# Pairing the stores of a batched matrix product: 6 KB runs by column-tiled products, and x issued two batches ahead

## The chip, the cores and the metric

One core of a Trainium2 chip. The metric is the device time of one execution in microseconds (us). Times are medians; every set of experiments has its own runs of the kernel before on the same chip, since chips and moments differ by about 0.1 us.

## The reference

```python
def setup_inputs():
    batch, dim_i, dim_j, dim_k = 32, 256, 512, 384
    # x: (32, 256, 512) float32,  y: (32, 512, 384) float32
def reference(x, y):
    return np.einsum('bij,bjk->bik', x, y).astype(np.float32)
```

x is 16.8 MB, y 25.2 MB and the result 12.6 MB. All of it has to pass the DMA engines once (the profile before: HBM read 41.94 MB, written 12.58 MB).

## The kernel before

x of four batches is loaded in one DMA (16 KB per partition), y of each batch in one DMA (6 KB per partition). PE, the matrix engine, transposes x; ACT and DVE, the scalar and the vector engine, cast the transposes and y to fp16; PE multiplies; ACT and DVE copy the products out, and the result of each batch leaves in a DMA of its own: 128 partitions, two rows of 1.5 KB each, a run of 3 KB. All DMAs are issued by SP, the sync engine, in program order (`eng` below is SP for every batch). The 16 DMA engines work a DMA off in packets; here each run of contiguous bytes is one packet (32 stores of 128 runs give the 4,096 packets of 3 KB in the trace). Each DMA adds 16 packets of 4 bytes, called completions here (1,152 for the 72 DMAs of the trace, with a median record of 9 ns).

```python
    def load(b):
        if b % Q == 0:                       # Q = 4
            x_of[b // Q] = x_pool.tile([P, R, J], F32, name="x_sb")
            keep(nc.sync.dma_start(out=x_of[b // Q],
                 in_=x[b : b + Q].rearrange("g (p r) j -> (g p) r j", r=R)))
        y_of[b] = y_pool.tile([P, NJ, K], F32, name="y_sb")
        keep(nc.sync.dma_start(out=y_of[b], in_=y[b].rearrange("(q t) k -> q t k", q=P)))
    ...
    def multiply(b):                         # two tiles of 128 rows, four products each
        ...
                keep(nc.tensor.matmul(ps_of[b][e], xt_sb[:, t, e].rearrange("c p h -> c (p h)"),
                                      y_r[:, t], start=(t == 0), stop=(t == NJ - 1)))
    ...
    def store(b):
        keep(eng.dma_start(out=out[b].rearrange("(m e) k -> m e k", m=P), in_=o_of.pop(b)))
    ...
    for s in range(B + 2):                   # one batch a stage
        if s + ahead < B: load(s + ahead)
        if s >= 2:        collect(s - 2)
        if 1 <= s <= B:   multiply(s - 1)
        if s < B and s % Q == 0: transpose(s // Q)
        if s < B:         round_y(s)
        if s >= 2:        store(s - 2)
```

## Time and profile before

| | before |
|---|---|
| time, median (range) | 136.25 us (136.09 to 136.34) |
| span of the profiled run (its device time) | 134.7 us (136.52 us) |
| busy: PE, ACT, DVE | 66%, 59%, 55% |
| DMA queue: packets, share of 16 engines | 10,368, 97.9% |
| mean DMA rate over the span | 405 GB/s |

Two more views of the page are needed later: the groups of instructions (busy us, mean ns of one, idle time before and who ended it) and the DMA issues (count, KB each, median us from issue to landing).

```profile
L94 ACT CAST xt_sb<-t_ps 128x512 f16<-128x512 f32 x32 | 39.8, 1350 | 44.0 <-PE t_ps L84 43.9
L92 DVE CAST xt_sb<-t_ps 128x512 f16<-128x512 f32 x32 | 40.1, 1323 | 40.3 <-PE t_ps L84 40.2
...
L115 PE MATMUL o_ps<-y_r,xt_sb 128*128 128x384 f16 x256 | 46.3, 342 | 14.9 <-ACT y_r L102 14.9
...
y_sb<-in_y_dram SPq DMA_DIRECT2D x32, 768.0 KB, 15.1
x_sb<-in_x_dram SPq DMA_DIRECT2D x8, 2048.0 KB, 14.2
out_dram<-o_sb SPq DMA_DIRECT2D x32, 384.0 KB, 14.1
```

The casts of the transposes take 1.3 us each, the products come in 256 instructions of 128 weight columns, and a DMA lands some 14 to 15 us after its issue, which is a queue that is always full (97.9% of 16 engines' span).

### The profile page before, as it was taken

What the parts mean: (1) busy time and instruction counts of PE and PEld (TensorE: products, weight loads), DVE (VectorE), ACT (ScalarE), POOL (GpSimd) and SP (SyncE); (2) the same over time, 40 slices, a digit from 0 to 9 for tenths busy, and PEclk for the clock granted to TensorE, in tenths of its full rate; (3) what the DMA queues carried; (4) which work ended last, traced back from release to release, by engine and by line L of the source; (5) the groups of instructions that cost most, each with busy time, mean ns of one, the idle gap of its engine ahead of it and who ended that gap; (6) DMA issues with size and microseconds to landing.
All of it is one profiled execution on the core that took longest, in us unless ns stands there. A gap on an engine that the chain in (4) does not pass through costs nothing.

```text
span 134.7 us, 1539 instructions
## 1 busy us (share of the span) xinstructions
PE 89.5 (66%) x512; PEld 66.6 (49%) x512; DVE 73.7 (55%) x128; ACT 80.1 (59%) x129; POOL 0.7 (1%) x6
## 2 busy tenths in 40 slices
PE   0049499769677908949794983949459492794920
PEld 0048368644564408925492543936259360793510
DVE  0008855975397503873489340796228870378720
ACT  3007994996299602795479650699218990179910
POOL 2000000000000000000000000000000000000000
PEclk9999999999999985686999599599995999559995
DMA  5999999999999999999999999999999999999992
GB/s 131 399 413 423 447 412 416 416 434 414 404 422 451 425 399 424 421 435 437 400 416 430 438 425 410 421 418 454 407 409 425 433 440 402 421 421 413 412 410 84
DMA packets 10375, 54.62 MB, mean 405 GB/s; under 512 B 1152, under 2 KB 1152, under 8 KB 9344
## 3 DMA queue, kind: packets, MB, share of 16 engines
q1 hardware_dynamic: 10368, 54.53, 97.9%
q8 instruction: 4, 0.07, 0.2%
q14 instruction: 3, 0.02, 0.0%
HBM read 41.94 MB, written 12.58 MB: 405 GB/s over the span
## 4 chain that ended last, share of the span: by engine, by line
DMA 79%; PE 8%; ACT 5%; DVE 2%; issue 2%; SPq 1%; DVEq 0%
DMA y_sb<-in_y_dram 30%; DMA x_sb<-in_x_dram 27%; DMA out_dram<-o_sb 21%; PE o_ps L115 4%; PE t_ps L84 4%; ACT xt_sb L94 2%; ACT y_r L102 2%; DVE xt_sb L92 1%; DVE y_r L104 1%; DVE o_sb L130 0%; SPq L69 0%; ACT o_sb L128 0%; SPq L63 0%; DVEq L130 0%
## 5 line engine op out<-in xcount | busy, mean ns | idle before, releaser
L94 ACT CAST xt_sb<-t_ps 128x512 f16<-128x512 f32 x32 | 39.8, 1350 | 44.0 <-PE t_ps L84 43.9
L92 DVE CAST xt_sb<-t_ps 128x512 f16<-128x512 f32 x32 | 40.1, 1323 | 40.3 <-PE t_ps L84 40.2
L84 PE MATMUL t_ps<-identity,x_sb 128*128 128x128 f32 x256 | 43.4, 340 | 24.5 <-DMA x_sb<-in_x_dram 24.3
L115 PE MATMUL o_ps<-y_r,xt_sb 128*128 128x384 f16 x256 | 46.3, 342 | 14.9 <-ACT y_r L102 14.9
L84 PEld LDWEIGHTS t_ps<-identity,x_sb 128*128 128x128 f32 x256 | 41.1, 216 | 27.8 <-issue 26.4
L115 PEld LDWEIGHTS <-xt_sb 128*128 128x128 f16 x256 | 26.2, 102 | 34.2 <-issue 19.9
L102 ACT CAST y_r<-y_sb 128x384 f16<-128x384 f32 x64 | 30.2, 527 | 0.6 <-DMA y_sb<-in_y_dram 0.6
L130 DVE COPY o_sb<-o_ps 128x384 f32<-128x384 f32 x32 | 17.8, 556 | 15.1 <-PE o_ps L115 15.1
L104 DVE CAST y_r<-y_sb 128x384 f16<-128x384 f32 x64 | 19.9, 354 | 0.4 <-DMA y_sb<-in_y_dram 0.4
L128 ACT COPY o_sb<-o_ps 128x384 f32<-128x384 f32 x32 | 15.4, 483 | 3.8 <-PE o_ps L115 3.8
L94 ACT ACT_TABLE_LOAD x1 | 1.3, 1283 | 0.7 <-PEq L168 0.7
masks.py:199 POOL TENSOR_SCALAR_AFFINE_SELECT identity<-identity 128x128 f32<-128x128 f32 x1 | 0.3, 294 | 0.1
masks.py:197 POOL MEMSET identity<- 128x128 f32 x1 | 0.2, 205 | 0.3 <-POOLq L168 0.3
L168 POOL MEMSET const-bfloat16-1.0<- 128x1 bf16 x1 | 0.1, 102 | 0.0
L168 POOL MEMSET const-uint8-127<- 128x1 uint8 x1 | 0.1, 102 | 0.0
L168 POOL MEMSET const-float32-0.0<- 128x1 f32 x1 | 0.1, 99 | 0.2 <-issue 0.2
L168 POOL MEMSET const-float32-1.0<- 128x1 f32 x1 | 0.1, 99 | 0.0
## 6 DMA issues: line engine op xcount, KB each, us to landing
y_sb<-in_y_dram SPq DMA_DIRECT2D x32, 768.0 KB, 15.1
x_sb<-in_x_dram SPq DMA_DIRECT2D x8, 2048.0 KB, 14.2
out_dram<-o_sb SPq DMA_DIRECT2D x32, 384.0 KB, 14.1
```

What stands on the lines that cost most here:

```text
L84: nc.tensor.transpose(t_ps[:, h].rearrange("c g p -> c (g p)"), x_sb[:, h * NI + e, t::NJ], identity,)
L92: keep(nc.vector.tensor_copy(dst, t_ps))
L94: keep(nc.scalar.copy(dst, t_ps))
L102: keep(nc.scalar.copy(yr_of[b][:, t], y_sb[:, t]))
L104: keep(nc.vector.tensor_copy(yr_of[b][:, t], y_sb[:, t]))
L115: nc.tensor.matmul(ps_of[b][e], xt_sb[:, t, e].rearrange("c p h -> c (p h)"), y_r[:, t], start=(t == 0), stop=(t == NJ - 1),)
L128: keep(nc.scalar.copy(o_of[b][:, e], ps_of[b][e]))
L130: keep(nc.vector.tensor_copy(o_of[b][:, e], ps_of[b][e]))
L168: nc = _bacc.Bacc("TRN2", target_bir_lowering=False, num_devices=1)
```

## The change

The intent: put the results of two batches side by side in the partitions (64 rows of one batch in partitions 0 to 63, 64 rows of the other in 64 to 127), so that one partition holds four rows of one batch, and a store of two batches has 6 KB runs. For that a product may give only 64 rows, so it is column-tiled: the two batches use the two halves of PE's columns. x is issued two batches ahead of the y that needs it, and transposed in two halves.

```diff
+G = 2
-LAG = 8
+LAG = 4                      # now counts pairs of batches
...
+    M = P // G               # 64 rows of each batch
+    NE = I // M
...
-        for e in range(NI):
-                    nc.tensor.matmul(ps_of[b][e], xt_sb[:, t, e] ..., y_r[:, t], ...)
+        for e in range(NE):
+            o_ps = opsum_pool.tile([P, K], F32, name="o_ps")
+            for t in range(NJ):
+                for g in range(G):
+                    nc.tensor.matmul(o_ps[g * M : (g + 1) * M],
+                        xt_sb[:, t, e, a * PQ : (a + 1) * PQ] ..., y_r[:, g, t], ...)
...
-        keep(eng.dma_start(out=out[b].rearrange("(m e) k -> m e k", m=P), in_=o_of.pop(b)))
+            nc.sync.dma_start(
+                out=out[u * G : (u + 1) * G].rearrange("g (m e) k -> (g m) e k", e=NE),
+                in_=o_of.pop(u))
...
+        if (u + 1) * G % Q == 0 and u + 1 < U:
+            load_x((u + 1) * G // Q)        # two batches ahead of its y
...
-    for s in range(B + 2):
+    for s in range(U + 2):                  # one pair of batches a stage
```

More of the change, by code (lines that the diff above doesn't have):

```diff
@@ L15 @@
 Q = 4
-LAG = 8
-ON_ACT = ()
+G = 2
+LAG = 4
 @with_exitstack
@@ L33 @@
     _, _, K = y.shape
-    NI = I // P
+    M = P // G
+    NE = I // M
     NJ = J // P
-    R = Q * NI
     PQ = P // Q
+    R = I // PQ
+    H = R // NE
+    U = B // G
     const_pool = ctx.enter_context(tc.tile_pool(name="const", bufs=1))
     x_pool = ctx.enter_context(tc.tile_pool(name="x_pool", bufs=3))
-    y_pool = ctx.enter_context(tc.tile_pool(name="y_pool", bufs=10))
-    yr_pool = ctx.enter_context(tc.tile_pool(name="yr_pool", bufs=4))
+    y_pool = ctx.enter_context(tc.tile_pool(name="y_pool", bufs=5))
+    yr_pool = ctx.enter_context(tc.tile_pool(name="yr_pool", bufs=2))
     xt_pool = ctx.enter_context(tc.tile_pool(name="xt_pool", bufs=2))
-    o_pool = ctx.enter_context(tc.tile_pool(name="o_pool", bufs=10))
+    o_pool = ctx.enter_context(tc.tile_pool(name="o_pool", bufs=5))
     tpsum_pool = ctx.enter_context(tc.tile_pool(name="tpsum", bufs=4, space=bass.MemoryType.PSUM))
@@ L57, with load_x, load @@
     x_of, y_of, yr_of, xt_of, ps_of, o_of = {}, {}, {}, {}, {}, {}
-    def load(b):
-        if b % Q == 0:
-            x_of[b // Q] = x_pool.tile([P, R, J], F32, name="x_sb")
+    def load_x(q):
+        x_of[q] = x_pool.tile([P, R, J], F32, name="x_sb")
+        keep(
+            nc.sync.dma_start(
+                out=x_of[q],
+                in_=x[q * Q : (q + 1) * Q].rearrange("g (p r) j -> (g p) r j", r=R),
+            )
+        )
+    def load(u):
+        if u == 0:
+            load_x(0)
+        if (u + 1) * G % Q == 0 and u + 1 < U:
+            load_x((u + 1) * G // Q)
+        y_of[u] = y_pool.tile([P, G, NJ, K], F32, name="y_sb")
+        for g in range(G):
@@ L62, in load @@
             keep(
                 nc.sync.dma_start(
-                    out=x_of[b // Q],
-                    in_=x[b : b + Q].rearrange("g (p r) j -> (g p) r j", r=R),
-                )
-            )
-        y_of[b] = y_pool.tile([P, NJ, K], F32, name="y_sb")
-        keep(nc.sync.dma_start(out=y_of[b], in_=y[b].rearrange("(q t) k -> q t k", q=P)))
-    def transpose(q):
-        x_sb = x_of.pop(q)
-        xt_of[q] = xt_pool.tile([P, Q, NJ, NI, PQ, Q], MM_DT, name="xt_sb")
-        n = 0
-        for t in range(NJ):
-            for e in range(NI):
-                t_ps = tpsum_pool.tile([P, Q, Q, PQ], F32, name="t_ps")
-                for h in range(Q):
-                    keep(
-                        nc.tensor.transpose(
-                            t_ps[:, h].rearrange("c g p -> c (g p)"),
-                            x_sb[:, h * NI + e, t::NJ],
-                            identity,
-                        )
-                    )
-                dst = xt_of[q][:, :, t, e].rearrange("c g p h -> c h g p")
+                    out=y_of[u][:, g],
@@ new lines, in load, with transpose @@
+                    in_=y[u * G + g].rearrange("(q t) k -> q t k", q=P),
+                )
+            )
+    def transpose(q, half):
+        x_sb = x_of[q]
+        if half == 0:
+            xt_of[q] = xt_pool.tile([P, NJ, NE, Q * PQ, H], MM_DT, name="xt_sb")
+        n = 0
+        for t in range(half * NJ // 2, (half + 1) * NJ // 2):
+            for e in range(0, NE, 2):
+                t_ps = tpsum_pool.tile([P, 2, H, Q * PQ], F32, name="t_ps")
+                for f in range(2):
+                    for h in range(H):
+                        keep(
+                            nc.tensor.transpose(
+                                t_ps[:, f, h], x_sb[:, h * NE + e + f, t::NJ], identity
+                            )
+                        )
+                dst = xt_of[q][:, t, e : e + 2].rearrange("c f p h -> c f h p")
@@ L95, in transpose @@
                 n += 1
-    def round_y(b):
-        y_sb = y_of.pop(b)
-        yr_of[b] = yr_pool.tile([P, NJ, K], MM_DT, name="y_r")
-        for t in range(NJ):
-            if t % 2 == 0:
-                keep(nc.scalar.copy(yr_of[b][:, t], y_sb[:, t]))
-            else:
-                keep(nc.vector.tensor_copy(yr_of[b][:, t], y_sb[:, t]))
-    def multiply(b):
-        xt_sb, y_r = xt_of[b // Q][:, b % Q], yr_of.pop(b)
-        ps_of[b] = [
-            opsum_pool.tile([P, K], F32, name=f"o_ps_{e}", tag="o_ps")
-            for e in range(NI)
-        ]
-        for t in range(NJ):
-            for e in range(NI):
-                keep(
-                    nc.tensor.matmul(
-                        ps_of[b][e],
-                        xt_sb[:, t, e].rearrange("c p h -> c (p h)"),
-                        y_r[:, t],
-                        start=(t == 0),
-                        stop=(t == NJ - 1),
-                    )
-                )
@@ L124, in collect, with round_y @@
-    def collect(b):
-        o_of[b] = o_pool.tile([P, NI, K], F32, name="o_sb")
-        for e in range(NI):
-            if e % 2 == 0:
-                keep(nc.scalar.copy(o_of[b][:, e], ps_of[b][e]))
-            else:
-                keep(nc.vector.tensor_copy(o_of[b][:, e], ps_of[b][e]))
-        del ps_of[b]
-    def store(b):
-        eng = nc.scalar if b in ON_ACT else nc.sync
-        keep(eng.dma_start(out=out[b].rearrange("(m e) k -> m e k", m=P), in_=o_of.pop(b)))
+    def round_y(u):
+        y_sb = y_of.pop(u)
+        yr_of[u] = yr_pool.tile([P, G, NJ, K], MM_DT, name="y_r")
+        for g in range(G):
+            for t in range(NJ):
+                if t % 2 == 0:
+                    keep(nc.scalar.copy(yr_of[u][:, g, t], y_sb[:, g, t]))
+                else:
+                    keep(nc.vector.tensor_copy(yr_of[u][:, g, t], y_sb[:, g, t]))
@@ new lines, in multiply @@
+    def multiply(u):
+        xt_sb, y_r = xt_of[u * G // Q], yr_of.pop(u)
+        ps_of[u] = []
+        for e in range(NE):
+            o_ps = opsum_pool.tile([P, K], F32, name="o_ps")
+            ps_of[u].append(o_ps)
+            for t in range(NJ):
+                for g in range(G):
+                    a = (u * G + g) % Q
+                    keep(
+                        nc.tensor.matmul(
+                            o_ps[g * M : (g + 1) * M],
+                            xt_sb[:, t, e, a * PQ : (a + 1) * PQ].rearrange("c p h -> c (p h)"),
+                            y_r[:, g, t],
+                            start=(t == 0),
+                            stop=(t == NJ - 1),
+                        )
+                    )
@@ new lines, in collect, with store @@
+    def collect(u):
+        o_of[u] = o_pool.tile([P, NE, K], F32, name="o_sb")
+        for e in range(NE):
+            if e % 2 == 0:
+                keep(nc.scalar.copy(o_of[u][:, e], ps_of[u][e]))
+            else:
+                keep(nc.vector.tensor_copy(o_of[u][:, e], ps_of[u][e]))
+        del ps_of[u]
+    def store(u):
+        keep(
+            nc.sync.dma_start(
+                out=out[u * G : (u + 1) * G].rearrange("g (m e) k -> (g m) e k", e=NE),
+                in_=o_of.pop(u),
+            )
+        )
@@ L138 @@
     ahead = LAG - 2
-    for b in range(ahead):
-        load(b)
-    for s in range(B + 2):
-        if s + ahead < B:
+    for u in range(ahead):
+        load(u)
+    for s in range(U + 2):
+        if s + ahead < U:
             load(s + ahead)
+        if s == 0:
+            transpose(0, 0)
+            transpose(0, 1)
         if s >= 2:
             collect(s - 2)
-        if 1 <= s <= B:
+        if 1 <= s <= U:
             multiply(s - 1)
-        if s < B and s % Q == 0:
-            transpose(s // Q)
-        if s < B:
+        if s < U:
@@ L151 @@
             round_y(s)
+        for half in range(2):
+            q = (s + 1 - half) * G // Q
+            if (s + 1 - half) * G % Q == 0 and 0 < q < B // Q:
+                transpose(q, half)
         if s >= 2:
```

## The prediction

> **What bounds the kernel now.** I began with the page: the busy shares, the slices and the DMA queue.
>
> ```profile
> PE 89.5 (66%) x512; PEld 66.6 (49%) x512; DVE 73.7 (55%) x128; ACT 80.1 (59%) x129; POOL 0.7 (1%) x6
> ...
> DMA  5999999999999999999999999999999999999992
> GB/s 131 399 413 423 447 412 416 416 434 414 404 422 451 425 399 424 421 435 437 400 416 430 438 425 410 421 418 454 407 409 425 433 440 402 421 421 413 412 410 84
> DMA packets 10375, 54.62 MB, mean 405 GB/s; under 512 B 1152, under 2 KB 1152, under 8 KB 9344
> ...
> q1 hardware_dynamic: 10368, 54.53, 97.9%
> ...
> DMA 79%; PE 8%; ACT 5%; DVE 2%; issue 2%; SPq 1%; DVEq 0%
> ```
>
> No compute engine is busy for more than 66% of the span. The DMA engines show 9 in every slice from the second to the last but one, at 400 to 454 GB/s, and the packets of the one queue take 97.9% of 16 engines' span: 0.979 x 134.7 = 131.9 us of a 134.7 us span. So DMA **throughput** bounds the kernel. The chain of waits agrees (79% DMA). What remains outside is small: the packet records of the trace show the first packet at 1.74 us and the last packet's end at 133.58 us.
>
> Then I asked why the compute waits do not matter. The waits by engine:
>
> ```profile
> ACT xt_sb L94 <- PE t_ps L84: 43.9, 16, 8.7
> DVE xt_sb L92 <- PE t_ps L84: 40.2, 18, 9.8
> ...
> PE t_ps L84 <- DMA x_sb<-in_x_dram: 24.3, 7, 8.7
> ```
>
> PE waits 24.3 us for x, in 7 stretches of up to 8.7 us, and ACT and DVE wait for PE in turn. These waits look large, but while PE is idle the DMA row still shows 9: an idle engine below a saturated queue costs nothing. The table of stretches carries the number that matters here, how fast a queue full of one kind of packet runs:
>
> ```profile
> 9.00:13.00 4.00, 3.81 (x21) 3.62 (x19) 2.77 (x3) 2.02 (x2) 0.00 (x0) 1.00 1.02 427
> 124.00:130.00 6.00, 4.97 (x31) 2.77 (x29) 3.53 (x9) 4.50 (x11) 0.00 (x0) 1.00 1.03 414
> ```
>
> The last two columns are DMA share and GB/s. From 9 to 13 us only y moves, in 6 KB runs: 427 GB/s. From 124 to 130 us almost only stores move, in 3 KB runs: 414 GB/s. Both are full, at 1.02 and 1.03. The 3 KB stores are thus about 3% less efficient per byte, and they are 12.58 of 54.5 MB.
>
> [...] Its packet records give medians of 121 ns for 3,072 B, 234 ns for 6,144 B and 611 ns for 16,384 B. The slope is (611 - 234) / 10,240 = 0.0368 ns per byte, or 27.2 GB/s per engine and 435 for sixteen, and the rest is 234 - 0.0368 x 6,144 = 8 ns per packet. The same two numbers give 113 + 8 = 121 ns for a 3 KB store, so stores and loads obey one law. [...] Its weight loads for the products take 102 ns and lie under the products.
>
> **The change part by part.**
>
> *Stores.* Before: 32 DMAs of 128 runs of 3 KB, 4,096 packets, 4,096 x 121 ns / 16 = 31.0 us of all engines. After: 16 DMAs of 128 runs of 6 KB, 2,048 packets, 2,048 x 234 ns / 16 = 30.0 us. Saved: 1.0 us. The stretches give the same: 12.58 MB / 414 - 12.58 MB / 427 = 30.4 - 29.5 = 0.9 us. Sixteen DMAs fewer also take 16 x 16 = 256 of the 4-byte completion packets away, at 9 ns: 256 x 9 / 16 = 0.14 us. The sum of packet time goes from 131.95 to about 130.9 us. Bytes and load runs (16 KB for x, 6 KB for y) stay. This part lies wholly on the path, because the path is this sum.
>
> *Products.* 256 products of 128 weight columns become 512 of 64 columns, each still streaming 384 columns. The timeline has 32 products in 5.36 us at clock 1.0, 167 ns each. For two batches that is 16 x 167 = 2.7 us now. After, 32 products: 2.7 us if the two halves of the array run side by side, 5.3 us if they run in turn. Transposes keep their number, 256; 32 of them take 4.5 us at full clock, so 2.2 us for a half group of 16. PE needs then 4.9 or 7.5 us per pair of batches. A pair's DMA time is about 130.9 / 16 = 8.2 us. Either way PE stays below the DMA, narrowly in the second case.
>
> *ACT and DVE.* The number and size of copies is the same: 64 of 128x512 from the transposes, 128 casts of y, 64 of 128x384 from the products. Only the stride in the transposed tile goes from 8 to 4 bytes. At 1.3 us per 128x512 those copies may get cheaper; they are off the path, so I count nothing.
>
> *Order of issue.* The instruction listing shows what the diff does not: a DMA waits for the landing of the eighth DMA before it, in both kernels. So at most eight are in flight. Four batches need 9 DMAs now (x, four y, four stores; 6.8 MB) and 7 after for the same bytes. Eight in flight are then 7.8 MB in place of 6.1, some 18.6 us of work at 420 GB/s in place of 14.4. The time from issue to landing will grow by that, with no harm, and a late store has more loads queued in front of it to hide behind. x lands two batches before the first y that needs it, so transposes, now in two halves, need no longer delay the products of their group. That should empty PE's wait for x, worth nothing in time as long as the queue is full.
>
> *The end.* After the last y lands, the queue has nine stores now (9 x 0.393 = 3.5 MB) and five after (3.9 MB, 9.4 us). The last store can go only when the last pair is cast (about 1 us after its second y), multiplied (2.7 to 5.3 us) and copied out (0.6 us): 4.3 to 6.9 us after landing, plus about 1 us from issue to first packet. The four stores before it keep the queue busy for 3.1 MB / 414 = 7.6 us. So it fits, with little to spare; at half clock, which some stretches show (0.50), it would not quite. I put 0.2 us on this.
>
> Sum: 136.25 - 1.0 - 0.14 + 0.2 = 135.3 us.
>
> **The rivals.**
>
> 1. *PE becomes the bound.* If column tiles ran in turn and their weight loads were no longer hidden (102 ns for 128 columns, so an estimated 51 for 64), a pair would cost 32 x (167 + 51) + 2,200 = 9.2 us against 8.2 of DMA: sixteen pairs take 147 us and the kernel some 155. For it: no trace here shows column tiles overlapping. Against it: today's weight loads do hide[...]. I give it 5%.
> 2. *The end opens up.* Last store twice as large, products at half clock: the DMA would run dry for 1 to 3 us and eat the gain: 136 to 138 us. For it: the half clock of 114 to 120 us. Against it: the clock was 1.00 in the last stretch, where PE had work.
> 3. *The earlier x is what helps.* PE's 24.3 us of waiting disappears; if compute were on the path, the time would fall by several us, to 131 or below. Against it: there is no slice with a slack DMA for it to fill, and 131.9 us of packets still have to pass.
> 4. *Stores are slower per byte than the law for loads says.* Writing 6 KB runs might gain nothing, leaving 136.2. Against it: the 3 KB stores already follow the law.
>
> **Range and chances.** The floor is 130.9 us of packets plus 1.7 before the first and some 1.1 to 2.5 after, and the 1.5 us by which the measured time exceeds the span: about 135.2 at best. Below 134.5 something else than packets would have to shrink. Above lie rivals 2 and 4. The range is 134.5 to 136.8. Faster by over 2% means below 133.5, less than the floor allows: 2%. Slower by over 2% is 139.0: rival 1 and the worst of rival 2, 6%.
>
> **What would show it.** 8,064 packets in the queue in place of 10,368, "under 8 KB" at about 7,040, the queue's packet time near 130.9 us, the DMA row at 9 throughout, the mean rate up by some 1%. Stores listed as 16 of 768 KB with landing times near 18 us. PE's wait for x near nothing. Products for a pair in 2.7 to 3.5 us would show the halves side by side; 5.3 us or more shows them in turn. I am wrong if the DMA row has holes in the middle (PE or an order of issue is then the bound), or if the last slices fall off earlier than the packet sum says, or if a 6 KB store packet takes much else than 234 ns.

## The result, and the profile after

| | before | after |
|---|---|---|
| time, median (range) | 136.26 us (136.09 to 136.47) | 136.12 us (135.92 to 136.59) |
| ratio | | 0.9995 (0.9975 to 1.0015) |
| ratio, a second set (after_again) | | 0.9979 (0.9964 to 0.9995) |
| span of the profiled run (its device time) | 134.7 us (136.52 us) | 134.3 us (136.04 us) |
| busy: PE, ACT, DVE | 66%, 59%, 55% | 66%, 48%, 42% |
| DMA queue packets | 10,368 | 8,064 |

The two profiled runs lie on opposite sides of their medians, so the spans overstate the difference. The time lies inside the predicted range, but hardly any of the predicted gain of 0.95 us came: 0.07 us by the first ratio, 0.29 by the second (0.0005 and 0.0021 of 136.3). The page of the changed kernel, the lines that answer to those shown of before:

```profile
PE 88.5 (66%) x768; PEld 73.2 (55%) x768; DVE 56.2 (42%) x128; ACT 63.9 (48%) x129; POOL 0.7 (1%) x6
...
DMA  5999999999999999999999999999999999999993
GB/s 112 415 400 450 409 417 421 456 388 421 417 448 408 409 428 421 457 394 417 413 443 436 408 417 428 442 422 402 425 423 444 426 402 427 419 427 419 417 394 158
DMA packets 8073, 54.65 MB, mean 407 GB/s; under 512 B 896, under 2 KB 896, under 8 KB 7040
...
q1 hardware_dynamic: 8064, 54.53, 97.8%
...
L130 PE MATMUL o_ps<-y_r,xt_sb 128*64 128x384 f16 x512 | 52.4, 364 | 28.5 <-ACT o_sb L143 20.8
...
L107 ACT CAST xt_sb<-t_ps 128x512 f16<-128x512 f32 x32 | 22.4, 731 | 23.6 <-PE t_ps L99 23.6
L105 DVE CAST xt_sb<-t_ps 128x512 f16<-128x512 f32 x32 | 22.6, 728 | 24.1 <-PE t_ps L99 23.8
...
y_sb<-in_y_dram SPq DMA_DIRECT2D x32, 768.0 KB, 17.9
x_sb<-in_x_dram SPq DMA_DIRECT2D x8, 2048.0 KB, 20.8
out_dram<-o_sb SPq DMA_DIRECT2D x16, 768.0 KB, 17.8
```

The packets are exactly those foretold, but not their summed time: by the packet records it fell from 131.95 to 131.37 us, by 0.58 in place of 1.14. Part of the difference is in the loads: a 16 KB packet took 630 ns on average after 625. The DMA row is full throughout, the queue is longer (17.8 to 20.8 us to landing), and ACT and DVE became cheaper: the casts of the transposes fell from 1.3 to 0.73 us. None of that shows in the time. The number to look at is the rate. The table of stretches, for the kernel before and then the changed one; the last two columns are DMA share and GB/s:

```profile
36.00:124.00 88.00, 62.87 (x349) 47.26 (x349) 52.10 (x89) 55.04 (x87) 0.00 (x0) 0.84 1.02 423
124.00:131.00 7.00, 4.97 (x31) 2.77 (x29) 3.53 (x9) 4.50 (x11) 0.00 (x0) 1.00 1.03 412
```

```profile
36.00:124.00 88.00, 62.95 (x541) 51.18 (x542) 40.24 (x93) 44.79 (x93) 0.00 (x0) 0.90 1.01 423
124.00:131.00 7.00, 4.41 (x55) 3.49 (x50) 2.77 (x6) 3.01 (x8) 0.00 (x0) 1.00 0.98 405
```

From 36 to 124 us loads and stores are mixed in the queue. Both kernels move 423 GB/s there (422.1 and 422.5 by the packet records of the data queue alone). Summing the packet records, both have the same 3.35 MB left at 124 us. After that only stores remain, and there the changed kernel is even a little slower, 405 against 412 GB/s, because some DMA engines wait for its last store: by the packet records only 9 to 14 of 16 are at work from 129.4 to 130.0 us. (This end varies: the trace of after_again has 374 GB/s there.) So the gain over the kernel before did not get lost later: in the long mixed stage it never arose.

### The profile page after: what moved, and what is told of

It is laid out like the page before. It is cut to its first block, busy times and chain, and to the rows that moved or that the text cites. A ratio compares the mean times of both kernels' runs of the same rounds, so it can differ in the third digit from the quotient of the medians.

```text
span 134.3 us, 1968 instructions
## 1 busy us (share of the span) xinstructions
PE 88.5 (66%) x768; PEld 73.2 (55%) x768; DVE 56.2 (42%) x128; ACT 63.9 (48%) x129; POOL 0.7 (1%) x6
## 3 DMA queue, kind: packets, MB, share of 16 engines
q1 hardware_dynamic: 8064, 54.53, 97.8%
HBM read 41.94 MB, written 12.58 MB: 406 GB/s over the span
## 4 chain that ended last, share of the span: by engine, by line
DMA 78%; PE 13%; ACT 4%; DVE 0%; issue 0%
DMA y_sb<-in_y_dram 40%; DMA x_sb<-in_x_dram 38%; PE o_ps L130 9%; PE t_ps L99 3%; ACT xt_sb L107 2%; ACT y_r L116 1%; ACT o_sb L143 1%; DVE o_sb L145 0%
## 5 line engine op out<-in xcount | busy, mean ns | idle before, releaser
L130 PE MATMUL o_ps<-y_r,xt_sb 128*64 128x384 f16 x512 | 52.4, 364 | 28.5 <-ACT o_sb L143 20.8
L130 PEld LDWEIGHTS <-xt_sb 128*64 128x64 f16 x512 | 39.1, 121 | 38.8 <-issue 22.4
L116 ACT CAST y_r<-y_sb 128x384 f16<-128x384 f32 x64 | 29.5, 514 | 38.7 <-DMA y_sb<-in_y_dram 38.6
L99 PE MATMUL t_ps<-identity,x_sb 128*128 128x128 f32 x256 | 36.9, 301 | 11.4 <-DMA x_sb<-in_x_dram 11.4
L99 PEld LDWEIGHTS t_ps<-identity,x_sb 128*128 128x128 f32 x256 | 34.1, 211 | 16.0 <-issue 16.0
L107 ACT CAST xt_sb<-t_ps 128x512 f16<-128x512 f32 x32 | 22.4, 731 | 23.6 <-PE t_ps L99 23.6
L105 DVE CAST xt_sb<-t_ps 128x512 f16<-128x512 f32 x32 | 22.6, 728 | 24.1 <-PE t_ps L99 23.8
L145 DVE COPY o_sb<-o_ps 128x384 f32<-128x384 f32 x32 | 16.3, 544 | 2.1 <-PE o_ps L130 2.1
L143 ACT COPY o_sb<-o_ps 128x384 f32<-128x384 f32 x32 | 13.9, 492 | 1.3 <-PE o_ps L130 1.3
## 6 DMA issues: line engine op xcount, KB each, us to landing
x_sb<-in_x_dram SPq DMA_DIRECT2D x8, 2048.0 KB, 20.8
out_dram<-o_sb SPq DMA_DIRECT2D x16, 768.0 KB, 17.8
```

The costliest lines, as they stand in the source:

```text
L99: nc.tensor.transpose(t_ps[:, f, h], x_sb[:, h * NE + e + f, t::NJ], identity)
L105: keep(nc.vector.tensor_copy(dst, t_ps))
L107: keep(nc.scalar.copy(dst, t_ps))
L116: keep(nc.scalar.copy(yr_of[u][:, g, t], y_sb[:, g, t]))
L130: nc.tensor.matmul(o_ps[g * M : (g + 1) * M], xt_sb[:, t, e, a * PQ : (a + 1) * PQ].rearrange("c p h -> c (p h)"), y_r[:, g, t], start=(t ...
L143: keep(nc.scalar.copy(o_of[u][:, e], ps_of[u][e]))
```

## The experiments

Fifteen kernels ran, in four sets. First theory (**additive law**, the prediction's): each store packet of 3 KB takes 121 ns and each of 6 KB 234 ns of an engine. Rivals: the records overlap, and the real cost is less (**overlap**); the order of loads and stores matters more than the run length (**order**); the changed kernel computes too late at its **end**; and, formed after the third set, the packet cost is real but is **hidden in the mixture** of loads and stores.

### Transfers alone

All computing is taken out; every store sends one constant tile, so results are wrong. Loads, stores and their order stay.

```diff
-        if s >= 2: collect(s - 2)
-        ... multiply, transpose, round_y ...
+        if s >= 2:
+            o_of[s - 2] = o_fix
             store(s - 2)
```

> The transfers of the kernel before alone, in their order, no computing; the stores send one constant tile, so the result is wrong on purpose. If the DMA queue alone sets the time (bandwidth theory), this is within 0.5 us of the kernel before, 135.8 to 136.3 us. If compute makes holes in the queue (rival), it is faster by over 1 us.

> The transfers of the changed kernel alone. Law of additive packet time (as predicted: 121 ns for 3 KB, 234 ns for 6 KB, 9 ns for a completion): 1.1 to 1.2 us below the transfers of before alone. Overlap theory (a packet's record overlaps the next one, real pitch of a 3 KB store 119 ns): only some 0.5 us below. Tail theory (the changed kernel loses its gain by computing late at its end): this kernel, which computes nothing, is 0.5 to 1 us below the changed kernel's 136.1.

Measured: dma_before 135.08 us, ratio 0.9904 (0.9886 to 0.9922); dma_after 135.68 us, ratio 0.9958 (0.9936 to 0.9981). Taking all computing away gives 1.3 us to the kernel before and 0.3 to 0.5 to the changed one (0.9958 against 0.9979 and 0.9995), so the DMA queue sets some 99% of the time. But 1.3 us is more than the 0.5 us that the bandwidth theory allowed; it lies on the rival's side (over 1 us), and it is more than the whole gain that was predicted: computing does cost the kernel before a little. Of the 1.0 us between the two profiled runs, 0.4 us built up by 124 us (422.1 GB/s in the mixed stage against 423.9), the rest later. What the additive law and the overlap theory expected did not come: with 2,304 packets fewer, the changed transfers are 0.6 us slower, not faster. The tail theory's 0.5 to 1 us was just missed too. Two more kernels part the two things that differ, the place of x and the pairing of the stores.

```diff
 dma_ahead_3k: loads of dma_after, stores of dma_before
+        for q in [0] * (b == 0) + [(b + 2) // Q] * (b % Q == 2 and b + 2 < B):
+            (load x of q)
 dma_quad_6k: loads of dma_before, and every second batch
+            nc.sync.dma_start(out=rows.rearrange("(m e) k -> m e k", m=P), in_=o_of.pop(b))  # 512 rows, 6 KB runs
```

> Transfers alone, loads in the order of before (x at the start of its four batches), stores in pairs with 6 KB runs. If the pairing of stores is what made the transfers of the changed kernel 0.6 us slower than those of before, this is slow too: 135.6 us or more. If the place of x is, this is as fast as or faster than the transfers of before: 134.5 to 135.1.

> Transfers alone, x two batches ahead as in the changed kernel, stores of one batch with 3 KB runs after each y as in before. If the place of x costs, 135.6 us or more; if the pairing of stores does, 135.1.

Measured: dma_quad_6k 135.60 us, 0.9957 (0.9940 to 0.9974); dma_ahead_3k 134.97 us, 0.9904 (0.9887 to 0.9922). For transfers alone the place of x does nothing; the pairing of the stores costs the 0.6 us. A third kernel keeps the order of the changed kernel (two y, then the pair's store) but sends the store as two DMAs of 3 KB runs.

> Transfers alone, order of the changed kernel (y y then the pair's store), but the store as two DMAs of 3 KB runs. If the pairing (order) costs: 135.6 or more, as the transfers of the changed kernel. If the 6 KB run itself or the 768 KB store costs: 135.0, as the transfers of before.

Measured: 135.80 us, 0.9970 (0.9951 to 0.9990). So it is the order that costs, not the 6 KB run. Where? The stretches of dma_ahead_3k, of dma_pair_3k and of dma_after:

```profile
36.00:124.00 88.00, 0.00 (x0) 0.00 (x0) 1.00 1.02 424
```

```profile
36.00:124.00 88.00, 0.00 (x0) 0.00 (x0) 1.00 1.02 422
```

```profile
36.00:124.00 88.00, 0.00 (x0) 0.00 (x0) 1.00 1.01 423
```

By the packet records these are 424.1, 422.5 and 423.7 GB/s; dma_before has 423.9. (Traces of nearly the same kernel differ by up to 0.3: the changed kernel has 422.5 and 422.3.) So with 3 KB runs the paired order loses 1.6 GB/s, or 0.3 us of the 88; with 6 KB runs almost nothing is lost here, and the rest must come at the end. There dma_ahead_3k and dma_after have 0.249 and 0.256 MB left at 131 us, the same; but the last packet ends at 132.06 us in one and at 132.68 in the other. In between, only a part of the 16 engines is at work: the DMA share of the 3 us from 131 us on is 0.20 and 0.17, which is 0.60 us of all 16 in the 1.06 us of dma_ahead_3k and 0.51 us in the 1.68 us of dma_after. An uneven finish of the engines makes the difference between these two traces. That the pairing makes the finish uneven is not shown: dma_before, which alternates, ended at 132.56 with 0.263 MB left (in the slowest of its six runs), and dma_mix_1k5 below, which pairs, ended 0.4 us after its last 0.740 MB were due at its 401 GB/s, against 1.1 us for dma_after at 427. The next kernel asks if the size of the last stores makes the finish uneven: dma_after, its last five stores in halves.

> Transfers alone as in the changed kernel, only the last five stores, after the last load, in halves of 3 KB runs. If the uneven end of the 16 engines comes from the size of the last stores: 0.3 to 0.6 us below 135.6. If it has built up before: 135.6.

Measured: 136.17 us, 0.9987 (0.9969 to 1.0005): not faster, and by the ratios 0.4 us slower than dma_after, though on another chip and with overlapping intervals. A miss. Why the engines finish unevenly stays open; the trace does not name the engine of a packet.

### The run length within the whole kernels

before_6k is the kernel before with stores of two batches in 6 KB runs (rows in wrong places); after_3k_one and after_3k_two are the changed kernel with 3 KB runs, in one DMA per pair (rows in wrong places) or in two (right result); after_again is the changed kernel as control.

```diff
 after_3k_two, store:
+   out=out[u*G:(u+1)*G].rearrange("g (m e) k -> (g m) e k", e=NE)[:, :2], in_=o_of[u][:, :2]
+   ... the same for [:, 2:]
 after_3k_one, store:
+   out=out[u*G:(u+1)*G].rearrange("g (m e) k -> g m e k", e=2).rearrange("g m e k -> m g e k")
 before_6k, store, for every second batch b:
+   out=rows.rearrange("(m e) k -> m e k", m=P)     # rows: the 512 rows of two batches
```

> The changed kernel, its stores still one DMA for two batches, but in 3 KB runs (rows in wrong places on purpose). Additive law: 1.0 us slower than the changed kernel, 137.1. Overlap theory: 0.3 to 0.6 us slower. If run length is worth nothing: equal.

> The changed kernel with two DMAs of 3 KB runs per pair of batches, right result: all packets as before, schedule and products as after. Additive law: 1.15 us slower than the changed kernel. Overlap theory: 0.4 to 0.7 us slower. Slower than the kernel before by over 0.3 us would show that the rest of the change costs time.

> The changed kernel once more, as the control of this set, with five rounds: ratio to the kernel before 0.999 +- 0.002 again. The additive law would have 0.992.

> The kernel before with one change: two batches' results leave in one DMA with 6 KB runs (rows in wrong places on purpose; products, loads and their order as before). Additive law: 1.15 us faster than before, ratio 0.9915. Overlap theory (3 KB store costs 119 ns of its engine, not 121, so two are 238 against 234): 0.4 to 0.6 us faster, 0.996. Order theory (stores that alternate with single loads run better than pairs of loads and bulk stores): no gain or a loss, 0.999 to 1.003.

| kernel | runs | median us | ratio (95%) |
|---|---|---|---|
| changed (after_again) | 6 KB | 136.01 | 0.9979 (0.9964 to 0.9995) |
| after_3k_one | 3 KB | 136.40 | 0.9996 (0.9980 to 1.0013) |
| after_3k_two | 3 KB | 136.53 | 1.0009 (0.9993 to 1.0025) |
| before_6k | 6 KB | 136.36 | 1.0006 (0.9987 to 1.0024) |

Between the changed kernel (0.9995 and 0.9979, mean 0.9987) and its two 3 KB forms lie 0.0009 and 0.0022, that is 0.1 and 0.3 us; the intervals are about as wide, so 0.3 is an upper size rather than a sure one. The traces agree: by the packet records the mixed stage, from 36 to 124 us, runs at 422.5 and 422.3 GB/s with 6 KB runs (changed kernel, after_again) and at 421.5 and 421.2 with 3 KB runs, which is 0.2 us of the 88. The additive law asked for 1.0 and 1.15 us, the overlap theory for 0.3 to 0.7. In the kernel before, 6 KB runs bring nothing, as the order theory had it, but before_6k is no clean test. Its mixed stage is faster than that of the kernel before (423.3 against 422.1 by the records), and its end is slower (348 against 412 GB/s):

```profile
36.00:124.00 88.00, 61.10 (x354) 47.34 (x353) 52.84 (x89) 55.68 (x89) 0.00 (x0) 0.88 1.01 424
124.00:131.00 7.00, 5.64 (x27) 2.87 (x25) 3.31 (x8) 3.72 (x9) 0.00 (x0) 0.82 0.84 348
```

And after_3k_two, which has every packet of the kernel before but all the rest of the change, takes the same time as the kernel before: column tiling, the new casts, the early x and the paired order together neither cost nor gain. Whether each does nothing is not shown. For transfers alone the paired order cost 0.9 us (0.9970 against 0.9904), so another part may have won that back; no run parts them.

### The end, and the alternating order with computing

after_alt has the changed kernel's computing, with each half of a pair's result stored after one y load, as in the quick order of the transfers alone. after_tail2 only cuts the last store in two.

```diff
 after_alt:
+        for g in range(G):
+            load(s + ahead, (g,))
+            ... collect(s - 2) when g == 0
+            store_half(s - 2, g)
 after_tail2:
+        if s == U + 1:
+            store_half(s - 2, 0)
+            store_half(s - 2, 1)
```

> The changed kernel's products, copies and early x, but each pair's result stored as two halves of 3 KB runs, each half after one y load, as the kernel before alternates them. Additive law: 1.15 us slower than the changed kernel, 137.2. Order theory (run length is worth nothing, fine alternation of loads and stores gives a shorter end): 0.3 to 0.7 us faster than the changed kernel, 135.3 to 135.7, and so faster than both.

> The changed kernel, only its very last store cut in two halves, the first of which may go when half of the last pair is copied out. Tail theory (DMA engines stand idle for about 1 us before the last store): 0.2 to 0.6 us faster than the changed kernel. If the end is not what it lost, equal.

Measured: after_alt 136.53 us, 1.0023 (1.0009 to 1.0036); after_tail2 136.03 us, 0.9988 (0.9974 to 1.0002). Neither the order theory nor the tail theory came; only "equal" for after_tail2 did. The order that is quick for transfers alone is not when computing is there. The trace of after_alt shows a late end: its last store is issued at 130.7 us, after 129.06 in the changed kernel, and the rate from 124 to 131 us is 389 GB/s, against 415 for dma_ahead_3k. Whether that is all of the cause was not tested.

```profile
124.00:131.00 7.00, 5.39 (x64) 4.39 (x64) 4.32 (x11) 4.68 (x11) 0.00 (x0) 1.00 0.99 389
```

after_tail2 did fill the gap at the end:

```profile
124.00:131.00 7.00, 4.07 (x51) 3.21 (x46) 2.61 (x6) 2.68 (x7) 0.00 (x0) 1.00 1.01 417
```

417 GB/s against the changed kernel's 405, yet the time is that of the changed kernel (0.9995 and 0.9979). Its last packet ends at 132.89 us, against 132.93. So filling the gap gained nothing here. That the engine that ends last was not one of those that idled in it would explain this, but it is not shown.

### Is the packet cost real?

Two kernels keep loads and stores apart: first all loads, then all stores, in 3 KB or in 6 KB runs. A third keeps the mixed order of dma_after but stores in 1.5 KB runs.

```diff
 dma_apart_*:
-        if s >= 2: store(s - 2)
+    for u in range(U): store(u)                # after all loads
 dma_mix_1k5, store:
+   out=out[u*G:(u+1)*G].rearrange("g i k -> (g i) k").rearrange("(h p) k -> p h k", p=P)
```

> Transfers alone, first all loads, then all stores, in 3 KB runs. Stores run some 30.3 us at 415 GB/s at the end. Hidden-in-mixture theory: 0.8 to 1.0 us slower than the same with 6 KB runs, and the loads alone run at about 418 GB/s, below the 423 of the mixture, so over 136.0. No-fixed-cost theory: equal to 6 KB.

> The same with 6 KB runs, two batches per store. Hidden-in-mixture theory: stores at 425 to 427 GB/s, 0.8 to 1.0 us faster than with 3 KB. No-fixed-cost theory: equal.

> Transfers alone in the mixed order of the changed kernel, stores in 1.5 KB runs (8,192 store packets in place of 2,048; rows in wrong places). Additive law: 8 ns for each of 6,144 more packets, over 16 engines 3.1 us more than with 6 KB, 138.7. Hidden-in-mixture theory: still 422 to 424 GB/s from 36 to 124 us, and only the stores after the last load slower, so 0.3 to 1.0 us more, 136 to 136.6.

Measured: dma_apart_3k 135.78 us, 0.9964 (0.9949 to 0.9978); dma_apart_6k 135.11 us, 0.9912 (0.9899 to 0.9926); dma_mix_1k5 136.20 us, 1.0005 (0.9987 to 1.0024). Loads alone (8 to 96 us) and stores alone (104 to 128 us), of the 3 KB kernel and then of the 6 KB one:

```profile
8.00:96.00 88.00, 0.00 (x0) 0.00 (x0) 1.00 1.01 423
...
104.00:128.00 24.00, 0.00 (x0) 0.00 (x0) 1.00 1.03 415
```

```profile
8.00:96.00 88.00, 0.00 (x0) 0.00 (x0) 1.00 1.01 423
...
104.00:128.00 24.00, 0.00 (x0) 0.00 (x0) 1.00 1.01 424
```

The cost is real: kept apart, 6 KB runs save 0.67 us, a little under the 0.8 to 1.0 expected. The other half of that expectation failed: loads alone run at 423 GB/s, not 418, and the total stayed under 136.0. And dma_mix_1k5, mixed and then with only its last stores left:

```profile
36.00:124.00 88.00, 0.00 (x0) 0.00 (x0) 1.00 1.02 419
126.00:131.00 5.00, 0.00 (x0) 0.00 (x0) 1.00 1.06 401
```

1.5 KB stores alone run at 401 GB/s, but the mixture that holds them still moves 419, less than the 422 to 424 expected. The additive law asked for 138.7 us, the hidden-in-mixture theory for 136 to 136.6; measured were 136.2.

From these rates the real time of a packet on its engine follows: bytes x 16 / rate is 61.3 ns at 1.5 KB (401), 118.4 at 3 KB (415) and 231.8 at 6 KB (424). Each doubling saves 4 to 5 ns, so the fixed cost of a packet is, as an estimate from these three rates, about 4 to 5 ns, not 8. The records say 65, 121 and 234 ns: a record overlaps the next one by 2 to 4 ns. The DMA share of 1.03 in the 3 KB line says the same, for a share cannot exceed 1 without overlap.

And in the mixture the 3 KB stores cost less than alone. From the packet records, 9.02 of the 37.31 MB that dma_before moved from 36 to 124 us were stores. If these ran at 415 GB/s and the loads at 423, the mean would be 37.31 / (28.29 / 423 + 9.02 / 415) = 421.0 GB/s; 423.9 were measured (dma_ahead_3k 424.1), as much as with 6 KB stores (dma_after 423.7). In dma_before and dma_ahead_3k single stores alternate with single loads. In the paired order less is hidden: dma_pair_3k would have 421.0 as well; 422.5 were measured. For 1.5 KB, also paired, 9.03 of 36.95 MB at 401 would give 417.4; 419.9 were measured. So against 423.7 the mixture hides all of the packet cost of 3 KB stores that alternate, and about half of it in the paired order: 1.2 of 2.7 GB/s remain at 3 KB, 3.8 of 6.3 at 1.5 KB. These are estimates from the rates of stores and loads alone, good to some 1 GB/s. That the mixture hides cost is shown by single traces of several kernels that agree; by which mechanism is not.

## Why the prediction was right or wrong

- **What bounds the kernel: right.** The transfers of the two kernels alone take 135.1 and 135.7 us of 136.3 and 136.1. Even with nothing to compute, no kernel's median was below 134.97. But that idle engines below a full queue cost "nothing" was too strong: without computing the kernel before is 1.3 us faster.
- **Stores: wrong, and this is the step that failed**: "4,096 x 121 ns / 16 = 31.0 us", "2,048 x 234 ns / 16 = 30.0 us", "Saved: 1.0 us", with 0.14 us for completions, and "This part lies wholly on the path, because the path is this sum." The path is not this sum. Two errors are in it. Records that overlap were added as if they stood one after the other: for stores kept apart the saving is 0.67 us, completions included, in place of 1.14. And a rate seen in a stretch of stores alone (414 GB/s) was given to all 12.58 MB, although 9 of them move beside loads, where the alternating 3 KB stores lose nothing (423.9 against 423.7 GB/s, transfers alone). Pairing the stores, which the 6 KB runs need, brings some of their cost back (422.5 GB/s), and the 6 KB run then takes that away again (423.7). So within the changed kernel, whose order is paired, the run length was worth 0.1 to 0.3 us, and against the kernel before next to nothing remains. The share of 1.03 stood in the very line from which I took 414.
- **Products: right.** In the timeline of the changed kernel, 32 products of 64 columns take as long (2.79 us) as 16 of 128 did (half of the 5.36 us for 32), so the halves of the array run side by side:

```profile
23.56 2.79 PE L130 MATMUL o_ps<-y_r,xt_sb 128*64 128x384 f16 x32 [1.85 <-ACT o_sb L143]
```

- 2.79 us, against 2.7 predicted for that case. Rival 1, PE as the bound, did not happen. Before this run no trace showed that the halves overlap; the 5% for rival 1 was my estimate.
- **ACT and DVE: right in direction.** The casts of the transposes fell from 1,323 (DVE) and 1,350 ns (ACT) to 728 and 731. Their fp16 results are written 4 bytes apart in place of 8, and the inner run grew from 32 to 128 elements; no run parts the two. That they are off the path agrees with after_3k_two (1.0009), which has them along with all the rest.
- **Order of issue: right on x and the landing times, but the order did matter.** Landing times of 17.8 to 20.8 us were foretold as some 18; in both traces at most eight DMAs were in flight, and 58 of 64 issues before and 42 of 48 after came within 0.2 us of the landing of the eighth DMA before them; PE's wait for x fell from 24.3 to 11.4 us, 8.7 of them the first load; dma_ahead_3k equals dma_before (0.9904 both), so the early x is worth nothing for transfers alone. That issuing the stores in pairs costs transfers alone 0.6 us was not foreseen.
- **The end: right in kind, too small in size, without effect on time.** The last y landed at 124.15 us and the last store was issued at 129.06, 4.9 us later, within the 4.3 to 6.9 predicted; the rate fell to 405 GB/s, 0.36 us of 7 at the 427 that 6 KB stores of dma_after reach in that stretch, against 0.2 predicted. Filling the gap changed nothing (after_tail2).
- **Rival 4** ("6 KB runs might gain nothing") was nearest to the outcome. I set it aside because "the 3 KB stores already follow the law", but the law was made of records, not of rates.
- **Small slips.** 131.95 less 1.14 is 130.8, not 130.9. The 1.5 us by which the time exceeds the span takes a median (136.25) and the span of a slower run (136.52); run by run it is 1.7 to 1.8. The second slice shows 399 GB/s, not 400.

The sum with measured terms: 0.1 to 0.3 us for the run length, about 0 for all the rest together, gives 136.0 to 136.2 us; measured 136.0 to 136.1. No version beat both kernels clearly: after_tail2 is only as good as the changed kernel.

Open: by which mechanism the mixture hides the packet cost, why paired stores make transfers alone slower, and whether the late end is all that keeps the alternating order, quickest alone, from paying with computing.

## What to carry to other kernels

Before you count a saving in DMA packet time, look whether the share of the queue exceeds 1 (1.03 here with 3 KB stores): then the records overlap, and bytes over time in a long stretch is the measure, not the sum of durations. Measure the rate in the stage that holds most of the traffic: 3 KB stores ran 2% slower than 6 KB stores alone (415 against 424 GB/s), and beside loads lost nothing or about half of that, depending on the order in which they were issued. A copy of the kernel without its computing tells in one run how much any change of the computing, or of waits, can still be worth with that order of transfers.
